# A chunked scan over two heads: from tiled products for each head to full-array products for a pair

## The chip, the core and the metric

The program runs on one core of one Trainium2 chip. The metric is the device time of one execution in microseconds. A core has TensorE (PE; its weight loads have a row of their own, PEld), VectorE (DVE), ScalarE (ACT), GpSimd (POOL) and SyncE (SP), each of which works through its own queue in order. SP, and in one place GpSimd, issue the DMAs.

## What is computed

Two decoder layers of width 2048 run over one sequence of 256 tokens. The first layer's token mixer is an RWKV-7 time mix with 32 heads of 64 channels, the second's is a convolution module; each is followed by a gated MLP. The change lies in the time mix, in the scan over tokens, which is cut here to its core:

```python
def step(S, inp):
    r_t, w_t, k_t, v_t, a_t, b_t = inp
    sa = jnp.einsum('bhij,bhj->bhi', S, a_t)
    S = (S * w_t[:, :, None, :] + sa[..., None] * b_t[:, :, None, :]
         + v_t[..., None] * k_t[:, :, None, :])
    y = jnp.einsum('bhij,bhj->bhi', S, r_t)
    return S, y
_, ys = lax.scan(step, S0, (r, decay, k, v, a, b))   # 256 steps, 32 heads
```

The state S is 64x64 for each head. Everything is float32.

## The kernel before

The kernel does the scan by chunks: 256 tokens are four chunks of 64 (`L`, `NC_`), and inside a chunk the recurrence is a triangular system, which is solved with matrix products. A tile of 128 partitions holds a **pair of heads**, head 0 in partitions 0 to 63 and head 1 in 64 to 127; there are 16 pairs.

Ahead of the scan the small triangular matrices of all heads (`dN`) are loaded by a GpSimd DMA (line 582), inverted in 32x32 blocks on VectorE (`inv_step`), and written back as `dT` and `dTn` by GpSimd DMAs (lines 640, 644). Meanwhile TensorE computes the first eight value tiles (`v_tile`). In the scan three kinds of work are interleaved:

- **Preparation of a pair** (`prep_gen`). For each chunk, one stationary operand holds the b and k vectors of both heads, and is multiplied with each head's a and r vectors (line 699, with the other head's rows zero) and with the identity (line 700, which gives the transpose). ScalarE copies a corner (`n21`, line 701) and the transpose (`tk`, line 706) out, VectorE masks the rest (line 704, 705). Then come eight 32x32 products `n21` by `tn` (line 714), eight centring products of the values, 64 columns at a time (line 733), and eight 32x32 products into the inverse's off-diagonal block (line 742). A bonus product follows (line 748). Each 32x32 or 64-column product uses a part of the array, which is chosen by where its operands and its output lie.
- **The chain of a pair** (`chain_gen`), chunk after chunk: W (line 762, a product for each head with 64 output rows), a ScalarE copy of W, the triangular product of both heads (line 775, full array), two ScalarE copies into `uv` (line 777), the state's update (line 781, one product for each head, then VectorE at line 161 or 786), and two contributions to the output y (lines 770 and 788, one product for each head). Each float32 product of a row is two instructions in the profile.
- **Filler**: value tiles 8 to 15 (`v_gen`, lines 244 to 246, three products of 256 columns for each of 16 blocks, from weights that ScalarE and GpSimd split into two parts), normalisation (`gn_gen`, tiled products at 798 and 816), first tiles of the output projection (`wo_gen`), and background jobs (`ada`, line 210, on VectorE, from weights of 1 MB).

PE's order is written by hand: a heap of generators, each with a due time, `PD` = 13 units a pair; the chains of two pairs and the preparation of a third are under way at a time. The other engines' orders are set by a scheduler. Loads of a pair (`prep_load`, `prep_load2`) stand on SP one pair ahead: `ari` (a and r, one tile for each head, zeros in the other head's partitions), `bk`, `tt` and `tn`. The zeros of `ari` that preparation overwrites are set again by GpSimd (line 765).

## Time and profile before

| | us |
|---|---|
| median of 3 runs | 2658.42 (2649.9 to 2659.04) |
| the profiled execution | 2656.6 |
| its span, first to last instruction | 2654.8 |
| the stretch from 400 to 720 us, in which the scan lies | 320 |
| PE busy in that stretch | 276.55 |
| VectorE / ScalarE / GpSimd busy in that stretch | 230.78 / 171.61 / 139.29 |
| granted TensorE clock, mean over the span | 0.975 |

In the PE timeline a row gives the start of the first instruction, the time to the end of the last, and a count. Ends overlap the next start, so what an instruction occupies is read from start to start. `128*64` ahead of the operands' shapes is the part of the array, rows by columns, that a product takes.

### The profile page before, as it was taken

The page shows a single profiled execution, that of the slowest core. Times are in us where ns is not written, and L with a number is a line of the kernel's source. Part 1 is how long each engine was busy: PE and PEld are TensorE (multiplying, and loading weights), DVE is VectorE, ACT ScalarE, POOL GpSimd, SP SyncE. Part 2 cuts the span into 40 slices and gives each one's busy share as a digit, 9 for nine tenths or more (in the row PEclk, how much of TensorE's full clock was granted, in tenths as well). Part 3 has the DMA queues.
Part 4 walks back from the last instruction along what each step waited for, and adds up shares of the span by engine and source line. Part 5 has one row for each costly group of instructions (what it writes and reads, how often), then busy time and mean ns, then how long its engine had stood idle before and what let it go on. Part 6 is the DMA issues. An engine that isn't in the chain of part 4 may idle for free.

```text
span 2654.8 us, 45461 instructions
## 1 busy us (share of the span) xinstructions
PE 2490.2 (94%) x17378; PEld 2202.6 (83%) x17378; DVE 2053.5 (77%) x3763; ACT 1363.4 (51%) x2636; POOL 507.2 (19%) x484
## 2 busy tenths in 40 slices
PE   5899997988999999999999989978999999999997
PEld 3688886877798888888888779967888888888886
DVE  4567767777678889889888989979998866666666
ACT  4565623565656543554455445544575445544554
POOL 0000016554002012002100248964320000000000
PEclk8999998999999999999999989979999999999999
DMA  8887766777275778888877854445767855555553
GB/s 316 323 319 277 202 214 213 230 222 231 98 270 218 283 282 340 299 295 300 323 289 286 289 201 159 160 143 213 265 237 279 282 197 187 179 191 190 191 178 124
DMA packets 154778, 630.37 MB, mean 237 GB/s; under 512 B 60480, under 2 KB 72256, under 8 KB 95936
## 3 DMA queue, kind: packets, MB, share of 16 engines
q1 hardware_dynamic: 153824, 624.85, 66.3%
q8 instruction: 136, 2.23, 0.3%
q0 software_dynamic: 736, 2.62, 0.3%
q14 instruction: 82, 0.67, 0.1%
HBM read 614.30 MB, written 13.11 MB: 236 GB/s over the span
## 4 chain that ended last, share of the span: by engine, by line
PE 71%; DVE 13%; DMA 9%; ACT 3%; issue 2%; POOL 1%; SPq 1%; DVEq 0%; ACTq 0%; POOLq 0%
PE ps L241 28%; PE ps L242 14%; PE ps L244 6%; PE ps L246 6%; PE ps L245 6%; DMA raw<-ada 5%; DVE raw L210 4%; DVE s L161 2%; DVE lo L234 2%; PE ps L379 1%; PE ps L307 1%; DVE s L158 1%; POOL lo L234 1%; ACT hi L233 1%; DVE s L155 1%
## 5 line engine op out<-in xcount | busy, mean ns | idle before, releaser
L241 PE MATMUL ps<-s,hi 128*128 128x512 f32 x3872 | 1357.5, 395 | 1.3 <-DVE s L155 1.1
L233 ACT CAST hi<-raw 128x1024 fp32r<-128x1024 f32 (+6 forms) x873 | 768.8, 897 | 862.4 <-PE ps L241 450.8
L242 PE MATMUL ps<-s,lo 128*128 128x256 f32 x3872 | 1086.0, 281 | 11.7 <-DVE lo L234 11.5
L234 DVE TENSOR_TENSOR lo<-raw,hi 128x1024 fp32r<-128x1024 f32 (+4 forms) x639 | 750.5, 1177 | 302.7 <-ACT hi L233 300.3
L241 PEld LDWEIGHTS ps<-s,hi 128*128 128x128 f32 x3872 | 726.5, 188 | 169.6 <-DVE s L155 1.7
L242 PEld LDWEIGHTS ps<-s,lo 128*128 128x128 f32 x3872 | 730.5, 189 | 18.8 <-DVE lo L234 17.4
L244 PE MATMUL ps<-s,hi 128*128 128x256 f32 (+1 forms) x1712 | 503.8, 295 | 7.3 <-ACT hi L233 5.6
L246 PE MATMUL ps<-s,lo 128*128 128x256 f32 (+1 forms) x1712 | 491.0, 288 | 19.3 <-DVE lo L234 17.2
L234 POOL TENSOR_TENSOR lo<-raw,hi 128x512 fp32r<-128x512 f32 x234 | 342.9, 1490 | 817.4 <-ACT hi L233 775.2
L245 PE MATMUL ps<-s,hi 128*128 128x256 f32 (+1 forms) x1712 | 489.7, 286 | 0.0
L246 PEld LDWEIGHTS ps<-s,lo 128*128 128x128 f32 x1712 | 330.5, 193 | 26.7 <-DVE lo L234 19.9
L244 PEld LDWEIGHTS ps<-s,hi 128*128 128x128 f32 x1712 | 330.7, 193 | 16.2 <-ACT hi L233 7.6
L245 PEld LDWEIGHTS ps<-s,hi 128*128 128x128 f32 x1712 | 331.2, 193 | 3.7 <-issue 3.0
L210 DVE CUSTOM_DVE_ANT_0 raw<-raw,cb,par 128x1024 f32<-128x1024 f32 x156 | 209.3, 1342 | 73.5 <-DMA raw<-ada 72.2
L210 DVE CUSTOM_DVE_ANT_0 raw<-raw,cb,md 128x1024 f32<-128x1024 f32 x156 | 217.1, 1392 | 0.8
L161 DVE SCALAR_TENSOR_TENSOR s<-ps,par,s 128x239 f32<-128x239 f32 (+26 forms) x420 | 166.0, 456 | 1.8 <-ACT s L164 1.2
L1192 POOL TENSOR_TENSOR s<-s,t 128x256 f32<-128x256 f32 x6 | 4.1, 726 | 703.5 <-DVE t L334 703.5
L161 DVE SCALAR_TENSOR_TENSOR s<-ps,md,s 128x256 f32<-128x256 f32 x213 | 100.7, 479 | 24.5 <-PE ps L242 19.6
L161 DVE SCALAR_TENSOR_TENSOR t<-t,par,t 128x255 f32<-128x255 f32 (+1 forms) x172 | 84.4, 491 | 1.1
L158 DVE TENSOR_TENSOR s<-ps,cst 64x64 f32<-64x64 f32 (+2 forms) x208 | 48.1, 253 | 34.5 <-ACT n L701 23.7
L164 ACT ACTIVATE t<-t,par 128x256 f32<-128x256 f32 x118 | 67.8, 585 | 7.0 <-DVE t L152 3.4
L155 DVE TENSOR_TENSOR s<-t,s 128x256 fp32r<-128x256 f32 x150 | 67.8, 461 | 1.5
(208 smaller groups left out, 2433.8 us busy)
## 6 DMA issues: line engine op xcount, KB each, us to landing
raw<-w_up SPq DMA_DIRECT2D x172, 1024.0 KB, 4.9
raw<-ada SPq DMA_DIRECT2D x156, 1024.0 KB, 6.4
raw<-w_dn SPq DMA_DIRECT2D x64, 896.0 KB, 4.6
raw<-w_pw SPq DMA_DIRECT2D x48, 1024.0 KB, 4.8
raw<-w_rkv SPq DMA_DIRECT2D x38, 1024.0 KB, 5.9
raw<-ada_s SPq DMA_DIRECT2D x32, 1024.0 KB, 6.6
raw<-w_dn SPq DMA_DIRECT2D x32, 960.0 KB, 6.2
raw<-w_o SPq DMA_DIRECT2D x11, 1024.0 KB, 5.0
```

The source lines that it names most:

```text
L155: nc.vector.tensor_tensor(out=o, in0=x, in1=y, op=ALU.subtract)
L158: nc.vector.tensor_tensor(out=o, in0=x, in1=y, op=ALU.mult)
L161: nc.vector.scalar_tensor_tensor(out=o, in0=x, scalar=s, in1=y, op0=op0, op1=op1)
L164: nc.scalar.activation(out=o, in_=i, func=func, bias=bias, scale=scale)
L210: nc.vector.tensor_tensor_reduce(out=r[q], in0=r[q], in1=cb[:, q * w:(q + 1) * w], scale=1.0, scalar=mod(l, piece, f) if q else pc("ada_b" ...
L233: nc.scalar.copy(hi[:, s], v[:, s])
L234: (eng or nc.vector).tensor_tensor(out=lo[:, s], in0=v[:, s], in1=hi[:, s], op=ALU.subtract)
L241: nc.tensor.matmul(acc.rearrange("p (a t) -> p a t", a=2), lhsT=hi[:, c], rhs=x[:, :, :T], start=first, stop=False, skip_group_check=True)
L242: nc.tensor.matmul(acc[:, T:], lhsT=lo[:, c], rhs=x[:, 0, :T], start=False, stop=last, skip_group_check=True)
L244: nc.tensor.matmul(acc[:, :n], lhsT=hi[:, c], rhs=x[:, 0, :n], start=first, stop=False)
L245: nc.tensor.matmul(acc[:, :n], lhsT=hi[:, c], rhs=x[:, 1, :n], start=False, stop=False)
L246: nc.tensor.matmul(acc[:, :n], lhsT=lo[:, c], rhs=x[:, 0, :n], start=False, stop=last)
```

## The change

Both heads of a pair are put side by side in the columns of one operand, with zeros where a head's columns meet the other head's rows. So each pair of products becomes one product of 128x128, of which the two diagonal 64x64 blocks are read.

- `ari` now is one tile for a (both heads) and one for r, in place of one for each head. Each is loaded by two DMAs, of 256-byte pieces: four for a pair where there were two of 2-KB pieces.
- W, both y products and the state's product are one full-array product each. The results lie in different columns for the two heads, so the copy of W becomes two copies of 64x64, and the copy of y two of 64x256. The square of y (`sqs`) is taken of the copy.
- The line-714 and line-742 products become four full-array products each, of 64 and of 96 columns, on `z` and on `tn` with zeros (two static buffers each, where `tn` had three).
- The centring becomes four products of 128 columns, on two neighbouring chunks of v; the last takes chunks 3 and 0, which GpSimd copies side by side into `vw`. The copies into `uv` become three.
- GpSimd sets a 64x64 block of `uv` to zero for each head.
- The identity product of line 700 becomes a transposing instruction (`nc.tensor.transpose`).
- Two switches that chose ScalarE and GpSimd forms (`WACT`, `RKP`) go; the forms stay.

```diff
-    aris = [[slot512().rearrange("p (c j t) -> p c j t", c=NC_, j=2) for _ in range(2)] for _ in range(4)]
+    aris = [[slot512().rearrange("p (c h t) -> p c h t", c=NC_, h=2) for _ in range(2)] for _ in range(4)]
...
+    zs = [pool.tile([P, NC_, 2, L], F32, tag="z", bufs=2, name=nm("z")) for _ in range(2)]
+    tns = [pool.tile([P, NC_, 2, 32], F32, tag="tn", bufs=2, name=nm("tn")) for _ in range(2)]
+    for t in zs + tns:
+        nc.gpsimd.memset(t, 0.0)
...
         for h, hr in enumerate(hrs):
-            nc.sync.dma_start(out=ari[h][hr], in_=dAR[f, hr])
+            for j in range(2):
+                nc.sync.dma_start(out=ari[j][hr, :, h, :], in_=dAR[f, hr, :, j, :])
...
+        for h, hr in enumerate(hrs):
+            nc.gpsimd.memset(uv[hr, 0, h, :], 0.0)
...
-            for h in range(2):
-                nc.tensor.matmul(pg[:, h * P:(h + 1) * P], lhsT=bkc, rhs=ari[h][:, c].rearrange("p j t -> p (j t)"), start=True, stop=True, skip_group_check=True)
-            nc.tensor.matmul(pg[:, T:T + P], lhsT=bkc, rhs=ident, start=True, stop=True, skip_group_check=True)
-            nc.scalar.copy(n21[:, c], pgv[:, :, 0, 32:64])
+            for j in range(2):
+                nc.tensor.matmul(pg[:, j * P:(j + 1) * P], lhsT=bkc, rhs=ari[j][:, c].rearrange("p h t -> p (h t)"), start=True, stop=True, skip_group_check=True)
+            nc.tensor.transpose(out=pg[:, T:T + P], in_=bkc, identity=ident)
+            nc.scalar.copy(z[:, c, :, 32:64], pgv[:, 0, :, 32:64])
...
-                nc.tensor.matmul(py[r1, c * 32:c * 32 + 32], lhsT=n21[r0, c, h, :], rhs=tn[r0, c, :], start=True, stop=True, skip_group_check=True)
+            nc.tensor.matmul(py[:, c * L:c * L + L], lhsT=z[:, c].rearrange("p h t -> p (h t)"), rhs=tn[:, c].rearrange("p h t -> p (h t)"), start=True, stop=True, skip_group_check=True)
...
-                nc.tensor.matmul(pvt[orow, cs], lhsT=v[:, cs], rhs=cen[:, hr], start=True, stop=True, skip_group_check=True)
+        vw = pool.tile([P, P], F32, tag="vw", bufs=1, name=nm("vw"))
+        for i, c in enumerate((NC_ - 1, 0)):
+            nc.gpsimd.tensor_copy(vw[:, i * L:(i + 1) * L], v[:, c * L:c * L + L])
+        for c in range(NC_):
+            vc = v[:, c * L:c * L + P] if c < NC_ - 1 else vw
+            nc.tensor.matmul(pvt[:, c * P:(c + 1) * P], lhsT=vc, rhs=cen, start=True, stop=True, skip_group_check=True)
...
-                nc.tensor.matmul(py[r0, c * 32:c * 32 + 32], lhsT=ysb[r1, c, :], rhs=tt[r1, c, r1], start=True, stop=True, skip_group_check=True)
+            nc.tensor.matmul(pyv[:, c], lhsT=z[:, c].rearrange("p h t -> p (h t)"), rhs=tt[:, c, 32:P], start=True, stop=True, skip_group_check=True)
...
-            for h, hr in enumerate(hrs):
-                kr = slice(0, P) if c else hrs[1 - h]
-                nc.tensor.matmul(pch[hr, wc], lhsT=ari[h][kr, c, 0, :], rhs=uv[kr, c, h, :], start=True, stop=True, skip_group_check=True)
+            nc.tensor.matmul(pch[:, wc], lhsT=flat(ari[0]), rhs=uvc, start=True, stop=True, skip_group_check=True)
...
-            (nc.scalar.copy if WACT else nc.vector.tensor_copy)(W, pch[:, wc])
+            for h, hr in enumerate(hrs):
+                nc.scalar.copy(W[hr], pw[hr, h])
...
-                for h, hr in enumerate(hrs):
-                    nc.tensor.matmul(psy[hr, cs], lhsT=uv[:, c, h, :], rhs=ari[h][:, c, 1, :], start=True, stop=False, skip_group_check=True)
+                nc.tensor.matmul(psy[:, cs], lhsT=uvc, rhs=flat(ari[1]), start=True, stop=False, skip_group_check=True)
...
-                for h, hr in enumerate(hrs):
-                    nc.tensor.matmul(pch[hr, wc], lhsT=tk[:, h, c, :], rhs=uv[:, c, h, :], start=True, stop=True, skip_group_check=True)
+                nc.tensor.matmul(pch[:, wc], lhsT=tk[:, c], rhs=uvc, start=True, stop=True, skip_group_check=True)
...
-            for h, hr in enumerate(hrs):
-                nc.tensor.matmul(psy[hr, cs], lhsT=uv[:, c, h, :], rhs=gr[:, h, c, :], start=c == 0, stop=True, skip_group_check=True)
+            nc.tensor.matmul(psy[:, cs], lhsT=uvc, rhs=flat(gr), start=c == 0, stop=True, skip_group_check=True)
...
-        nc.scalar.copy(ycs[f], psy[:, :T])
-        act(sqs[f], psy[:, :T], AF.Square)
+        for h, hr in enumerate(hrs):
+            nc.scalar.copy(ch(ycs[f])[hr], psv[hr, :, h, :])
+        act(sqs[f], ycs[f], AF.Square)
```

The lines of the changed kernel are numbered otherwise: 766, 774, 779, 784 and 790 are the chain's products (before: 762, 770, 775, 781, 788); 718, 735 and 744 are the preparation's (before: 714, 733, 742); 772 is the copy of W (before: 767); 732 is the copy into `vw`. Outside the scan each engine's order stays as it was.

Order on PE, one place in the scan where two chains, the centring and a block product meet. `ps` is an accumulator, `s` a data tile, `cst` the constants, `t` a value tile. Before:

```order
L762 MATMUL ps_4979<-s_4715,s_3976 64x64
L762 MATMUL ps_4979<-s_4715,s_3977 64x64
L770 MATMUL ps_4978<-s_3976,s_4715 64x64
L770 MATMUL ps_4978<-s_3977,s_4715 64x64
L733 MATMUL ps_5123<-cst,t_4126 64x64 x8
L762 MATMUL ps_4769<-s_4518,s_3974 64x64
L762 MATMUL ps_4769<-s_4518,s_3975 64x64
L770 MATMUL ps_4768<-s_3974,s_4518 64x64
L770 MATMUL ps_4768<-s_3975,s_4518 64x64
L742 MATMUL ps_5142<-s_3971,ys_5085 32x32 x8
L775 MATMUL ps_4979<-W_5117,s_3970 128x64
```

The same place in the changed kernel:

```order
L766 MATMUL ps_4962<-s_4713,s_3976 128x128
L774 MATMUL ps_4961<-s_3977,s_4713 128x128
L735 MATMUL ps_5096<-cst,t_4144 128x128 x3
L735 MATMUL ps_5096<-cst,vw_5097 128x128
L766 MATMUL ps_4768<-s_4528,s_3974 128x128
L774 MATMUL ps_4767<-s_3975,s_4528 128x128
L744 MATMUL ps_5114<-s_3971,z_4001 128x96 x4
L779 MATMUL ps_4962<-W_5090,s_3970 128x64
```

The steps stand in the same sequence; 24 tiled products became 12 full-array ones.

Order on ScalarE, the copies of one chain step between two chunks of preparation (`Sp` is the scaled state, `n` is `n21`, `t` and the second `s` are other copies). Before:

```order
L767 COPY W_4753<-ps_4555 128x64
L706 COPY s_4714<-ps_4733 128x2x64
L767 COPY W_4772<-ps_4769 128x64
L701 COPY n_804_4716<-ps_4774 128x64
L777 COPY s_4355<-ps_4555 64x64 x2
```

The changed kernel:

```order
L772 COPY W_4752<-ps_4567 64x64 x2
L713 COPY s_4712<-ps_4733 128x128
L772 COPY W_4770<-ps_4768 64x64 x2
L708 COPY z_4000<-ps_4773 128x2x32
L781 COPY s_4374<-ps_4567 64x64 x2
```

Each copy of W is two copies in a row. Over the whole program ScalarE has 2734 instructions for 2638, GpSimd 565 for 489, SP 992 for 960, and VectorE 3765 as before.

Order on GpSimd around the inversion, from the last zeros of `ari` to the first write of `dTn`; the `lo` rows split the weights of a value tile. Before:

```order
L610 MEMSET s_3979 64x512
L582 DMA raw_3963<-dN 128x1024 x2
L234 ISA
L234 TENSOR_TENSOR lo_4381<-raw_4365,hi_4380 128x512 x2
L234 TENSOR_TENSOR lo_4429<-raw_4365,hi_4428 128x512 x2
L644 DMA dTn<-s_4338 128x512
```

The changed kernel:

```order
L610 MEMSET s_3979 64x4x64 x2
L732 COPY vw_4501<-t_4029 128x64 x2
L580 DMA raw_3963<-dN 128x1024 x2
L232 ISA
L232 TENSOR_TENSOR lo_4400<-raw_4384,hi_4399 128x512 x2
L232 TENSOR_TENSOR lo_4448<-raw_4384,hi_4447 128x512 x2
L649 DMA dTn<-s_4358 128x512
```

The copies of pair 0's value chunks now stand ahead of the load of `dN` on this queue.

## Rows read from the trace of the kernel before

**Rows 1.** The profile page: the span.
```profile
span 2654.8 us, 45461 instructions
```

**Rows 2.** Stretches of the scan: length, then busy us (instructions) of PE, PEld, DVE, ACT, POOL; clock.
```profile
460.00:500.00 40.00, 39.70 (x461) 35.64 (x461) 27.70 (x80) 23.89 (x87) 25.63 (x21) 1.00 0.76 250
...
580.00:620.00 40.00, 33.45 (x400) 26.25 (x397) 34.97 (x95) 26.19 (x96) 19.33 (x22) 0.96 0.66 214
...
400.00:720.00 320.00, 276.55 (x2949) 232.66 (x2947) 230.78 (x598) 171.61 (x590) 139.29 (x126) 0.94 0.61 198
```

**Rows 3.** PE in time order (start, length, line, shapes, count): the array in one form.
```profile
479.76 0.61 PE L699 MATMUL ps<-s,s 128*128 128x128 f32 x4
480.21 0.39 PE L700 MATMUL ps<-cst,s 128*128 128x128 f32 x2
480.35 0.37 PE L244 MATMUL ps<-s,hi 128*128 128x256 f32 x1
480.55 0.28 PE L245 MATMUL ps<-s,hi 128*128 128x256 f32 x1
```

**Rows 4.** PE in time order: the six trips of tiled products in one head pair's period.
```profile
475.57 0.28 PE L246 MATMUL ps<-s,lo 128*128 128x256 f32 x1
475.78 0.33 PE L762 MATMUL ps<-s,s 64*64 64x64 f32 x4
...
476.27 0.28 PE L245 MATMUL ps<-s,hi 128*128 128x256 f32 x1
...
477.10 0.28 PE L246 MATMUL ps<-s,lo 128*128 128x256 f32 x1
...
478.24 0.39 PE L700 MATMUL ps<-cst,s 128*128 128x128 f32 x2
...
482.96 0.28 PE L246 MATMUL ps<-s,lo 128*128 128x256 f32 x1
483.17 0.34 PE L781 MATMUL ps<-s,s 128*64 128x64 f32 x4
483.34 0.29 PE L788 MATMUL ps<-s,s 128*64 128x64 f32 x4
...
483.78 0.28 PE L245 MATMUL ps<-s,hi 128*128 128x256 f32 x1
...
484.25 0.28 PE L246 MATMUL ps<-s,lo 128*128 128x256 f32 x1
484.46 0.44 PE L714 MATMUL ps<-tn,n 32*32 32x32 f32 x16
...
485.43 0.28 PE L245 MATMUL ps<-s,hi 128*128 128x256 f32 x1
...
485.91 0.28 PE L246 MATMUL ps<-s,lo 128*128 128x256 f32 x1
...
486.40 0.92 PE L733 MATMUL ps<-cst,t 128*64 128x64 f32 x16
...
487.73 0.44 PE L742 MATMUL ps<-s,ys 32*32 32x32 f32 x16
...
488.38 0.65 PE L748 MATMUL ps<-t,cst 128*128 128x256 f32 x2
488.86 0.33 PE L775 MATMUL ps<-W,s 128*128 128x64 f32 x2
...
489.98 0.38 PE L699 MATMUL ps<-s,s 128*128 128x128 f32 x1
```

**Rows 5.** Who waited for whom, 440 to 720 us: total us, times, longest.
```profile
PEld ps L775 <- ACT W L767: 6.4, 10, 1.5
```

**Rows 6.** ScalarE in time order: a copy of W.
```profile
477.69 0.21 ACT L767 COPY W<-ps 128x64 f32<-128x64 f32 x1 [0.57 <-PE ps L762]
```

**Rows 7.** ScalarE's copies of the first v tiles: min/median/max ns, first and last start us.
```profile
L590 ACT COPY t<-ps x8: 372/372/373, 359.6 to 407.9; 128x256 f32<-128x256 f32 x8
```

**Rows 8.** GpSimd in time order: the load of dN, with which the inversion begins.
```profile
365.02 1.26 POOL L582 DMA_DIRECT2D raw<-dN  x2 [9.25 <-DMA dN<-s]
```

More of the change, by code (lines that the diff above doesn't have):

```diff
@@ L64 @@
 BGT2 = 7
-WACT = 1
 TQ = 2
@@ L70 @@
 GP = 8
-RKP = 1
 NG = 12
@@ L668, in prep_load2 @@
         tt = tts[f % 4]
-        tn = pool.tile([P, NC_, 32], F32, tag="tn", bufs=3, name=nm("tn"))
+        tn = tns[f % 2]
         for h in range(2):
@@ L674, in prep_load2 @@
                 nc.sync.dma_start(out=tt[r0:r0 + 32, :, r0:r0 + 32], in_=dT[rows, b].rearrange("c s t -> s c t"))
-            nc.sync.dma_start(out=tn[h * L:h * L + 32], in_=dTn[rows].rearrange("c s t -> s c t"))
+            nc.sync.dma_start(out=tn[h * L:h * L + 32, :, h, :], in_=dTn[rows].rearrange("c s t -> s c t"))
         ld[f] += (tt, tn)
@@ L726, in prep_gen @@
+            nc.gpsimd.tensor_tensor(out=ch(rk)[hr], in0=ch(rk)[hr], in1=ari[1][hr, :, h, :], op=ALU.mult)
         yield PU
         pvt = ps("g")
-        for h, hr in enumerate(hrs):
-            orow = hrs[1 - h]
-            for c in range(NC_):
-                cs = slice(c * L, c * L + L)
-                nc.tensor.matmul(pvt[orow, cs], lhsT=v[:, cs], rhs=cen[:, hr], start=True, stop=True, skip_group_check=True)
-        for h, hr in enumerate(hrs):
-            orow = hrs[1 - h]
-            nc.scalar.copy(uv[orow, :, h, :], ch(pvt[orow, :T]))
+        vw = pool.tile([P, P], F32, tag="vw", bufs=1, name=nm("vw"))
@@ L737, in prep_gen @@
+        nc.scalar.copy(uv[hrs[1], 0, 0, :], pvv[hrs[1], NC_ - 1, 0, :])
         yield PU
         py = ps("g")
+        pyv = py[:, :NC_ * 96].rearrange("p (c t) -> p c t", c=NC_)
         for c in range(NC_):
[L740 to L742 removed]
+            nc.tensor.matmul(pyv[:, c], lhsT=z[:, c].rearrange("p h t -> p (h t)"), rhs=tt[:, c, 32:P], start=True, stop=True, skip_group_check=True)
```

55 lines of the change are left out of this document (26 added, 29 removed).

## The prediction

> **What bounds the kernel now.** I read the page first: PE is the engine that sets the end of the whole program, and the span is 2654.8 us [rows 1]; the profiled execution took 2656.6. The change touches only the scan, so I next read busy time by stretch [rows 2]. From 400 to 720 us PE is busy 276.55 of 320. Two kinds of stretch are to be seen. From 460 to 500 PE is busy 39.70 of 40 at full clock: there every nanosecond that PE's own stream saves or costs moves the end. From 580 to 620 it is busy 33.45: there it waits for VectorE, which is itself busy 34.97 of 40 with chain steps and background jobs, and a shorter PE stream only waits longer. After the scan PE goes on without a break into weights that are loaded ahead, so what the scan gains or loses reaches the end whole.
>
> Then I read PE in time order, from start to start. In one array form the stream is regular: four line-699 instructions of 128 columns take 480.21 - 479.76 = 0.45, so 0.112 each, and the step from them to the next kind costs nothing: 480.21 to 480.55 is 0.34 for two of line 700 and the first of line 244, which is 2 x 0.112 + 0.118 [rows 3]. So a full-array product of 128 columns (two instructions) costs 0.224, and a 256-column instruction of the value tile 0.118.
>
> A tiled product between them costs more than its instructions. One line-762 pair alone, between 475.57 and 476.27, takes 0.70; less the two 0.118 of its neighbours this is 0.46 [rows 4]. Lines 781 and 788 together, 482.96 to 483.78, take 0.82 - 0.236 = 0.58. So a further pair of head products costs 0.12 (its four 64-column instructions run beside one another), and the trip out of the full array and back costs 0.46 - 0.12 = 0.34, whatever is done in it.
>
> **The change part by part.**
>
> *Products and trips.* I add up one head pair's period, from 475 to 490 us, in which PE never waits [rows 4]. It has six trips with 14 pairs of head products, eight and eight 32x32 products and eight centring products:
> - 475.57 to 476.27: 0.46, as above.
> - 477.10 to 478.24: 1.14, less 0.118 and less 4 x 0.112 for the line-699 instructions in it: 0.57.
> - 482.96 to 483.78: 0.58.
> - 484.25 to 485.43: 1.18 - 0.236 = 0.94 (the line-714 products stand in it).
> - 485.91 to 488.38: 2.47, less 0.118 and some 0.2 for the line-775 product in it: 2.15 (centring, line 742 and two chain steps).
> - 488.86 to 489.98: 1.12, less 0.2 for line 775: 0.92; the cost of the way back comes after the last row shown, some 0.1.
>
> Sum: 5.72 us a pair. After the change the same work is 14 products at 0.224 (3.14), four centring products at 0.224 (0.90), and the four products of 64 and four of 96 columns. No row has these two shapes with a full-width output in a stream of their own. By columns they are 0.112 and 0.168, and no more than the 0.224 of 128 columns; I take the middle, 0.17 and 0.19: 1.45. Sum 5.49, so **-0.23 a pair, -3.7 us** for 16. With the low ends it is -9.0, with the high ends +1.7.
>
> *Trips that stay.* The products of lines 798 and 816 remain tiled: 16 and five groups. By the PE timeline about nine of these 21 now share a trip with head products and will have one of their own: 9 x 0.34 = **+3.1 us**.
>
> *The transposing instruction.* There are 64, each now a product of 0.224. No transposing instruction is in this trace. The nearest rows: unchanged, 0.224; one instruction of 128 columns in place of two, 0.112; the rate of the value tile's instructions (256 columns in 0.118), 0.06. I take 0.112, which differs least from the row it replaces: **-7.2 us** (0 to -10.5). It could also be a change of form with a trip's price of 0.34 each: +21.8; that is a rival. A sentence apart: the Trainium skill ("TensorE: Matmul & The Clock Gate", Terms) says that transposing is four times faster for float32, by which this term would be an estimated -10.8, and the sum 3.6 lower.
>
> *The copies of W.* ScalarE now copies W in two steps; one copy is 0.21 [rows 6], and I take the same for one of half the partitions. W is what the chain's full-array product waits for, and behind that PE's whole stream. PE's loads were seen to wait for this copy 10 times [rows 5]; in the other 54 chunks filler hides it. So 10 x 0.21 = **+2.1 us**, between 0 and 64 x 0.21 = 13.4. In all ScalarE gets 96 more instructions, some 20 us at 0.21; it is busy 171.61 of 320 [rows 2], and the weight splits that queue behind are made a tile ahead, so I cost the rest at nothing; if the cover is gone it is the first rival below.
>
> *What is given back.* The PE terms add up to -7.8. About two thirds of the scan is like 580 to 620, where PE waits for others anyway; I let half of the gain there go into longer waits: **+2.6 us**. What is late there is VectorE's state update behind a background job, which the change does not touch: VectorE has the same 3765 instructions.
>
> *SP.* 32 more DMA issues, in smaller pieces. They stand a pair's period (15 us) ahead of their use, so nothing waits for them, and behind them on SP are weight loads, also a tile ahead: 0. With two `tn` buffers in place of three the load for pair f waits for pair f-2's first block product, done by then: 0.
>
> *GpSimd.* 32 copies into `vw`, 32 zeroings of `uv`, and zeroings at the start. Pair 0's copies stand ahead of the load of `dN`, with which the inversion begins, and behind that load is the whole scan. They wait for the first value tile, whose copy starts at 359.6 and takes 0.37 [rows 7]; the load was issued only at 365.02, after 9.25 of waiting for the writes of `dN` [rows 8]. So there are 5 us of cover: 0. If the value tile came later than 364, each microsecond of it would be one of the end. In the scan GpSimd is busy 139.29 of 320 [rows 2], and `vw` is needed by the centring only late in a preparation: 0.
>
> Sum: -3.7 + 3.1 - 7.2 + 2.1 + 2.6 = -3.1, so 2656.6 - 3.1 = 2653.5 on the profiled execution. That execution lies 1.8 below the median of the three runs, 2658.4; against the median the sum gives 2655.3. I forecast **2654**.
>
> **The rivals.**
>
> *All of it is cheap.* The transposing instruction at 0.06, the narrow products by their columns, W's second copy hidden: -9.0 + 3.1 - 10.5 = -16.4, if PE's gain is felt everywhere: 2640. For it speaks that a tiled trip also delays what the chain waits for; against it the stretches in which VectorE is late.
>
> *ScalarE becomes the bound of the chain.* If each of its 96 added copies is on the path (20.2) and transposing gains nothing: 20.2 - 3.7 + 3.1 = +19.6, 2676. It decides from the point where ScalarE is busy most of the time between two chain steps; it is busy 171.61 of 320 now, which speaks against it.
>
> *Transposing drains the array as a tiled product does.* 64 x 0.34 = +21.8, with -3.7 + 3.1 + 2.1: +23.3, 2680. It would show as a step of some 0.3 around each transposing row; nothing in this trace speaks for or against it.
>
> *The trip's price is not that of the form.* If the 0.34 stayed when the products fill the array (because the chain's operands cost it), the old work without trips is 5.72 - 6 x 0.34 = 3.68, the new 5.49: 1.81 x 16 = +29.0, less 7.2, plus 2.1: 2680. Against it: line 699 follows line 246 and line 244 follows line 700 at no price [rows 3]. Beside it, a sentence apart: the Trainium skill ("TensorEngine Tiling (Array Packing)", Theoretical Speedup and Key Properties) says that 64-wide tiles work in parallel for up to twice the speed, which speaks against this change, and that a switch of the tiling mode drains the array, which speaks for it; the trace agrees with both, 0.12 for two heads' products against 0.224, and 0.34 a trip.
>
> **How the numbers follow.** Half a per cent, 13 us, is about what a measurement of this kernel tells from no change: 2645 to 2672. The forecast's case, terms of either sign that nearly cancel, has 0.50. All cheap has 0.28 and is the case of faster by more than that. ScalarE 0.11, draining 0.08 and the trip's price 0.03 are the slower cases, 0.22. The range reaches from the cheap case, with 6 us beyond its centre for waits that shrink too, to the slower rivals' centres: 2634 to 2680; what is left out is some of either tail, under 2 in 10.
>
> **What would show it.** On PE's timeline the chain's products should stand at 0.22 with no step before or after; the `z` products between 0.11 and 0.22 each; the transposing row at 0.11. PE's busy share from 460 to 500 should stay near full with the pair's period of about 15 us shorter by 0.5. PE's waits for W should grow by about 2 us, and those for VectorE a little. The load of `dN` should be issued as soon after its writes as before. I am wrong if PE's waits in the scan change by more than 10 us either way, or if a step of 0.3 stands at each transposing row.

## The result, and the profile after the change

The changed kernel takes **2684.24 us** (median of four runs, 2675.34 to 2686.33) against 2658.39 for the kernel before: a ratio of 1.0101, with a 95% interval of 1.008 to 1.0122. Run again beside the experiments it came to 2679.82, ratio 1.0099 (1.0077 to 1.0121). It is slower by about 26 us. The forecast was 2654, with a range that ended at 2680, so the prediction was wrong in sign and just missed with its range.

The profiled execution took 2683.13 us. First its span and the stretches that answer to [rows 1, 2] (columns as there):

```profile
span 2681.4 us, 43888 instructions
```

```profile
460.00:500.00 40.00, 35.41 (x274) 33.23 (x272) 25.59 (x68) 23.42 (x87) 23.57 (x27) 0.96 0.68 220
580.00:620.00 40.00, 33.48 (x244) 30.35 (x243) 30.92 (x88) 26.52 (x107) 11.08 (x24) 0.91 0.65 205
400.00:720.00 320.00, 277.32 (x1980) 253.44 (x1979) 222.48 (x581) 184.28 (x653) 145.02 (x188) 0.93 0.63 201
```

From 460 to 500 us PE was busy 39.70 of 40 before and is now busy 35.41: the stretch that I took for one bound by PE alone has become one in which PE waits. Over 400 to 720 PE is as busy as before (277.32 against 276.55), but the scan is not over at 720.

To see both sides I cut the scan the same way in every trace, from pair 0's bonus product (line 748 before, 750 after) to the last product of W with the inverse (line 775 before, 779 after), and added up for each PE instruction the time to the start of the next, less the idle time that the trace shows between them. I call the sum PE's work in the scan.

| us in the scan | before | after | after, second execution |
|---|---|---|---|
| length | 265.6 | 284.6 | 280.4 |
| PE's work | 241.2 | 254.3 | 253.4 |
| of it, at the lower granted clock | 14.8 | 21.9 | 19.5 |
| PE's work, all at the higher clock (estimate) | 235.0 | 244.3 | 244.4 |
| PE idle | 24.4 | 30.3 | 27.1 |

The second execution is the changed kernel run again. The trace shows the clock granted to PE at one of two levels in each stretch, 1.2 or 2.4 GHz. Over the whole program the mean granted clock is the same, 0.974 against 0.975, but in the scan it is 0.966 before and 0.958 and 0.963 after. At the lower level an instruction of the same line and shape, with the same line behind it, occupied PE 1.7 to 1.9 times as long as at the higher; the estimate divides the work at the lower level by that (1.72 before, 1.83 and 1.85 after).

So 15 to 19 us of the loss lie in the scan: some 9 in PE's work as such, 3 to 4 in that more of it ran at the lower clock, 3 to 6 in idle time. With one execution of the kernel before, it isn't shown that the change itself brings the lower clock: in the scans of the runs below that have the background products, it lasts from 6 to 55 us. The rest of the loss lies ahead of the scan and behind it, where the executions shown here differ by several us anyway (pair 0's bonus product starts between 433.6 and 447.5 in them).

What PE waited for, 440 to 725 us (total us, times, longest), before and then after:

```profile
PE ps L762 <- DVE s L161: 5.5, 7, 1.7
PE ps L775 <- ACT W L767: 3.9, 7, 1.2
```

```profile
PE ps L766 <- DVE s L159: 16.4, 11, 4.4
PE ps L779 <- ACT W L772: 1.9, 4, 0.7
```

The wait for the copy of W, now in two steps, did not grow. The wait of the W product for VectorE's state update (line 161 before, 159 after) tripled; in the second execution it is 13.0. What stands ahead of that update is to be seen in VectorE's time order, after:

```profile
478.38 1.28 DVE L208 CUSTOM_DVE_ANT_0 raw<-raw,cb,par 128x1024 f32<-128x1024 f32 x1 [5.66 <-issue]
...
480.66 1.48 DVE L208 CUSTOM_DVE_ANT_0 raw<-raw,cb,md 128x1024 f32<-128x1024 f32 x1
482.06 0.08 DVE L208 DVE_READ_ACCUMULATOR2_ANT md<- 128x1 f32 x1
482.06 0.58 DVE L159 SCALAR_TENSOR_TENSOR s<-ps,plc,Sp 64x64 f32<-64x64 f32 x2
```

Line 208 is a background product: half of a modulation vector's dot product, which runs on VectorE beside the scan. VectorE stood idle 5.66 us at the head of one, then ran both halves, and only then the state update. The profile names no releaser for that wait (`issue`), but the load of these weights was issued at 472.76 and took 5.5 us to land. PE's W product is what waited:

```profile
482.70 0.56 PE L766 MATMUL ps<-s,s 128*128 128x128 f32 x2 [2.61 <-DVE s L159]
```

VectorE's waits ahead of such products, before and after (same columns as the waits above; 16.6 and 5.9 in the second execution):

```profile
DVE raw L210 <- DMA raw<-ada: 15.7, 15, 2.8
```

```profile
DVE raw L208 <- DMA raw<-ada: 24.4, 12, 5.4
...
DVE raw L208 <- issue: 10.5, 3, 5.7
```

Now the prices. PE in time order after, a stretch with weight tiles between the trips:

```profile
469.32 0.28 PE L244 MATMUL ps<-s,lo 128*128 128x256 f32 x1
469.44 0.39 PE L784 MATMUL ps<-s,s 128*128 128x128 f32 x2
469.66 0.39 PE L790 MATMUL ps<-s,s 128*128 128x128 f32 x2
469.81 0.36 PE L242 MATMUL ps<-s,hi 128*128 128x256 f32 x1
470.01 0.28 PE L243 MATMUL ps<-s,hi 128*128 128x256 f32 x1
...
470.48 0.28 PE L244 MATMUL ps<-s,lo 128*128 128x256 f32 x1
470.60 1.00 PE L718 MATMUL ps<-tn,z 128*128 128x64 f32 x8
471.44 0.44 PE L784 MATMUL ps<-s,s 128*128 128x128 f32 x2
471.71 0.39 PE L790 MATMUL ps<-s,s 128*128 128x128 f32 x2
471.85 0.36 PE L242 MATMUL ps<-s,hi 128*128 128x256 f32 x1
472.06 0.28 PE L243 MATMUL ps<-s,hi 128*128 128x256 f32 x1
```

State and y product of a chunk (lines 784, 790) between weight tiles: 469.32 to 470.01 is 0.69, against 0.82 in [rows 4] from 482.96 to 483.78, a gain as forecast. With the first y products beside them: 470.48 to 472.06 is 1.58, against 1.18 in [rows 4] from 484.25 to 485.43, a loss of 0.40, where the prediction's own prices make 0.18. Line 718 shows why: its eight instructions are 64 columns wide, and the next line starts 0.84 later, 0.105 each, nearly what 128 columns take.

### The profile page after: what moved, and what is told of

It reads as the page before. It is cut to its first block, busy times and chain, and to the rows that moved or that the text cites. A ratio compares the mean times of both kernels' runs of the same rounds, so it can differ in the third digit from the quotient of the medians.

```text
span 2681.4 us, 43888 instructions
## 1 busy us (share of the span) xinstructions
PE 2512.5 (94%) x16482; PEld 2234.6 (83%) x16482; DVE 2049.1 (76%) x3763; ACT 1387.0 (52%) x2732; POOL 517.5 (19%) x560
## 4 chain that ended last, share of the span: by engine, by line
PE 69%; DVE 13%; DMA 9%; ACT 3%; issue 3%; POOL 1%; SPq 1%; DVEq 0%; ACTq 0%; POOLq 0%
PE ps L239 27%; PE ps L240 14%; PE ps L242 6%; PE ps L244 6%; PE ps L243 6%; DMA raw<-ada 5%; DVE raw L208 4%; DVE lo L232 3%; DVE s L159 2%; PE ps L377 1%; ACT hi L231 1%; DVE s L156 1%; DMA raw<-w_dn 1%; POOL lo L232 1%; DVE s L153 1%
## 5 line engine op out<-in xcount | busy, mean ns | idle before, releaser
L244 PE MATMUL ps<-s,lo 128*128 128x256 f32 (+1 forms) x1712 | 491.6, 288 | 18.5 <-DVE lo L232 17.9
L232 POOL TENSOR_TENSOR lo<-raw,hi 128x512 fp32r<-128x512 f32 x234 | 336.0, 1460 | 816.9 <-ACT hi L231 759.1
L244 PEld LDWEIGHTS ps<-s,lo 128*128 128x128 f32 x1712 | 330.5, 193 | 26.3 <-DVE lo L232 20.8
L159 DVE SCALAR_TENSOR_TENSOR s<-ps,md,s 128x256 f32<-128x256 f32 x213 | 100.8, 480 | 30.3 <-PE ps L240 20.8
L162 ACT ACTIVATE t<-t 128x256 f32<-128x256 f32 x118 | 49.2, 417 | 55.1 <-DVE t L159 50.2
```

The lines of the kernel that those rows point to most:

```text
L159: nc.vector.scalar_tensor_tensor(out=o, in0=x, scalar=s, in1=y, op0=op0, op1=op1)
L162: nc.scalar.activation(out=o, in_=i, func=func, bias=bias, scale=scale)
L232: (eng or nc.vector).tensor_tensor(out=lo[:, s], in0=v[:, s], in1=hi[:, s], op=ALU.subtract)
L244: nc.tensor.matmul(acc[:, :n], lhsT=lo[:, c], rhs=x[:, 0, :n], start=False, stop=last)
```

## The experiments

Theory A: the loss is PE's work. Theory B: it is the order on VectorE, where a state update stands behind a background product that waits for its weights. Theory C: a full-width step takes longer from state to W and back. D: SP's extra issues. E: GpSimd, held by the one buffer of `vw`. Each ratio is against the kernel before, timed on the same chip.

### Each part alone, or put back alone

**The transposing instruction alone**, in the kernel before:

```diff
-nc.tensor.matmul(pg[:, T:T + P], lhsT=bkc, rhs=ident, start=True, stop=True, skip_group_check=True)
+nc.tensor.transpose(out=pg[:, T:T + P], in_=bkc, identity=ident)
```

> The kernel before with one edit: the product with the identity becomes a transposing instruction. Theory A (TensorE's work sets the scan): in the trace of the changed kernel the transposing takes 5.5 us in the scan where the product took 13.6, so 8 us less work for TensorE; if half to all of that reaches the end, 2650 to 2655 us against 2658. Theory B (the changed kernel is slow because background products on VectorE come ahead of the chain's state update, not because of TensorE's work): within 3 us of 2658, either way. Rival of the prediction (the transposing instruction drains TensorE): 2680.

2658.75 us, ratio 1.0011 (0.9994 to 1.0028). As B had it. PE's work in the scan fell by 5.6 us (its own line by 6.4) and idle time rose by 2.5; of the rest no gain is to be seen in the whole time. PE in time order there:

```profile
478.42 0.71 PE L699 MATMUL ps<-s,s 128*128 128x128 f32 x4
478.97 0.27 PE L700 MATMUL ps<-cst,s 128*128 128x128 f32 x1
479.00 0.37 PE L244 MATMUL ps<-s,hi 128*128 128x256 f32 x1
```

From the four of line 699 to the weight tile is 0.58, and five instructions of 0.112 would be 0.56: no step of 0.3 stands there.

**The changed kernel with its y products put back** into 32x32 tiles:

```diff
-nc.tensor.matmul(py[:, c * L:c * L + L], lhsT=z[:, c].rearrange("p h t -> p (h t)"), rhs=tn[:, c].rearrange("p h t -> p (h t)"), start=True, stop=True, skip_group_check=True)
+for h in range(2):
+    r0, r1 = slice(h * L, h * L + 32), slice(h * L + 32, h * L + 64)
+    nc.tensor.matmul(py[r1, c * 32:c * 32 + 32], lhsT=z[r0, c, h, 32:64], rhs=tn[r0, c, h, :], start=True, stop=True, skip_group_check=True)
...
-nc.tensor.matmul(pyv[:, c], lhsT=z[:, c].rearrange("p h t -> p (h t)"), rhs=tt[:, c, 32:P], start=True, stop=True, skip_group_check=True)
+for h in range(2):
+    r0, r1 = slice(h * L, h * L + 32), slice(h * L + 32, h * L + 64)
+    nc.tensor.matmul(py[r0, c * 32:c * 32 + 32], lhsT=z[r1, c, h, 0:32], rhs=tt[r1, c, r1], start=True, stop=True, skip_group_check=True)
...
```

> The changed kernel with the two y products of the preparation put back into 32x32 tiles of the array (z and tn keep their new layout). Theory A: over the scan these products take 15.7 + 15.0 us of TensorE's time after and took 7.1 + 7.0 before, so 16.6 us of work goes, and two of six trips per pair come back (16 pairs x 2 x 0.09 to 0.34 us = 2.9 to 10.9 us): 2684 - 6 to 14 = 2670 to 2678 us. Theory B: TensorE's work is not what counts, 2681 to 2688 us.

2669.47 us, ratio 1.0051 (1.0032 to 1.007): about half of the loss is gone. PE's work fell by 7.7 (y lines 14.9 less, 7.2 back elsewhere for two trips a pair). That is half a microsecond under A's band and far from B's: B alone is out.

**The changed kernel with centring put back** into half width, without `vw`:

```diff
-vw = pool.tile([P, P], F32, tag="vw", bufs=1, name=nm("vw"))
...
-    nc.tensor.matmul(pvt[:, c * P:(c + 1) * P], lhsT=vc, rhs=cen, start=True, stop=True, skip_group_check=True)
+for h, hr in enumerate(hrs):
+    orow = hrs[1 - h]
+    for c in range(NC_):
+        cs = slice(c * L, c * L + L)
+        nc.tensor.matmul(pvt[orow, cs], lhsT=v[:, cs], rhs=cen[:, hr], start=True, stop=True, skip_group_check=True)
...
```

> The changed kernel with the centring products of v put back into half-width products, two of 64 columns for a chunk, so that the wrap tile vw and its two GpSimd copies are gone. Theory A: centring took 14.6 us of TensorE's time before and 16.9 after, and two of six trips come back: 2684 give or take 5 (2680 to 2689). Theory B in the form that GpSimd, held by the single vw tile (20.8 us of waits for the centring product in the scan), makes the low halves of the weights and with them the next loads late: at least 8 us less, 2676 or under.

2668.72 us, ratio 1.0052 (1.0036 to 1.0068). A expected no change; B, in the form in which GpSimd is held by `vw`, expected 2676 or under. PE's work is only 2 us less, and that by the clock (by the estimate at the higher clock it is 1 more); its idle time is 7 less (23.1). So A alone is out too.

**The changed kernel with the chain put back** into half width:

```diff
-nc.tensor.matmul(pch[:, wc], lhsT=flat(ari[0]), rhs=uvc, start=True, stop=True, skip_group_check=True)
+for h, hr in enumerate(hrs):
+    kr = slice(0, P) if c else hrs[1 - h]
+    nc.tensor.matmul(pch[hr, wc], lhsT=ari[0][kr, c, h, :], rhs=uv[kr, c, h, :], start=True, stop=True, skip_group_check=True)
...
-for h, hr in enumerate(hrs):
-    nc.scalar.copy(W[hr], pw[hr, h])
+nc.scalar.copy(W, pch[:, wc])
...
```

The state product and both y products are put back in the same way.

> The changed kernel with the chain's products (W, y, state, y of u) put back into half-width products, W in one ScalarE copy and the output tile in its old layout; the preparation stays full-width. Theory A: these lines took 47.8 us of TensorE's time in the scan before and 58.0 after, so 10 us of work goes and two of six trips per pair come back (2.9 to 10.9 us): 2684 - 7 to +1 = 2677 to 2685 us. Theory B in the form that the chain's own steps (W's two copies, a state product that ends later) start the lag of the state updates: at least 12 us less, 2672 or under.

2665.01 us, ratio 1.0032 (1.0011 to 1.0054), in B's band. PE's work is not less at all (258.2 against 254.3; the chain's lines 9.4 less, the trips back, and 2 us more by the clock), but its idle time fell from 30.3 to 13.0. Against 2684 and 2680 the three edits give back 10 to 15, 11 to 16 and 15 to 19 us: their sum is far more than the whole loss, so the parts don't add up in the time.

**The chain alone** at full width, the preparation as before: the changed kernel with its y products, its centring and the product with the identity put back, by the diffs shown.

> Only the chain's four products take the full array (W, both y products, state), with W in two copies; y products, centring and the product with the identity are as in the kernel before. Theory A: the chain's lines took 9 us more of TensorE's time in the changed kernel, and the trips they saved come off, so 2658 + 5 to 12 = 2663 to 2670 us. Theory C: the idle time grows by 5 us or more on top of that, 2670 to 2677.

2668.55 us, ratio 1.0039 (1.0022 to 1.0055), where A put it. C isn't seen: PE's idle time in the scan, 21.3, is no longer than before.

**The new layout alone**: the changed kernel with its y products, its centring and its chain put back by the three diffs. The transposing instruction stays.

> Every full-width product is put back, and what is left of the change is the layout: ari's two tiles by use with both heads in each, four small loads of dAR per pair for two, tn in two buffers for three, tk's single copy, the memsets of uv, and the transposing instruction. Theory A: these cost nothing, within 4 us of the run with the transposing instruction alone, 2655 to 2663 us. Theory D (the queue of SP: four small loads take longer to issue, so later weights land late): 2665 us or more.

2654.52 us, ratio 0.9991 (0.9973 to 1.0009). SP's smaller loads, two `tn` buffers and the zeroings cost nothing that can be measured. D falls.

Taken at the higher clock by the same estimate, PE's work in the scan is 6.5 us less than before with the transposing instruction alone, 5.8 more with the chain alone, and 6.4 less with the new layout; against the changed kernel it is 8.4 less with the y products put back, 1.2 more with centring and 2.0 more with the chain.

### Without the background products

The kernels of this part leave 34 of the products out, so they compute less than the task.

```diff
-at(0, bg_gen(99))
+for l_, piece, f in jobs:
+    nc.gpsimd.tensor_copy(out=mod(l_, piece, f), in_=pc("ada_b", (l_ * 6 + piece) * KT + f))
...
+del jobs[:]
```

> The kernel before without the 34 modulation products (of the o gate and of the FFN's scale and shift) that run in the scan's background on VectorE, and without their 34 loads; their columns hold the bias alone. It is the base for the next run. From the first bonus product to the last u product the kernel before takes 265.6 us, of which TensorE is idle for 24.4; here, if VectorE's queue is what TensorE waits for, the idle time falls to 12 us or less.

> The same edit in the changed kernel, which leaves out the same 34 products and loads. With them the changed kernel took 284.6 us from the first bonus to the last u product (254.3 us of work for TensorE and 30.3 idle) against 265.6 (241.2 and 24.4). Theory A: the 13 us of work stay, and the two kernels differ by 11 to 16 us in this stretch. Theory B (order on VectorE): TensorE's idle time comes out equal in both, within 2 us, since nothing stands ahead of the state updates. Theory C (a full-width step takes longer from the state to W and back, so that TensorE waits on the chain itself): the changed kernel still idles 5 us or more longer than the one before.

| us in the scan, no background products | before | after |
|---|---|---|
| length | 239.0 | 249.1 |
| PE's work | 233.3 | 241.3 |
| PE idle | 5.7 | 7.8 |

PE's idle time before, 5.7, is less than half of the 12 that I allowed. The difference between the kernels fell from 15 to 19 us to 10: 8 of work, 2 of idle time. Waits for the state update all but vanish, after without background products:

```profile
PE ps L766 <- DVE s L159: 1.2, 3, 0.5
```

The difference is 1 us short of A's band, and the idle time grew by just the 2 us that B allowed. So theories A and B both hold a part, and C at most the 2 us of idle time. How far the scan hangs on the background products is to be seen in the chain of waits of the kernel before, which I had not read for this stretch (shares by line, 440 to 707 us):

```profile
by line: DMA raw<-ada 17.9%; DVE raw L210 14.0%; PE ps L244 4.9%; PE ps L699 4.6%; DVE s L158 3.7%; PE ps L811 3.5%; DMA s<-dAR 3.5%; PE ps L245 3.5%; PE ps L246 3.4%; issue 3.2%; PE ps L762 2.7%; DMA raw<-w_o 2.6%; PE ps L775 2.6%; PE ps L
```

and without the background products (438 to 678 us):

```profile
by line: PE ps L699 13.0%; PE ps L244 11.3%; PE ps L245 7.7%; PE ps L246 7.6%; PE ps L775 6.1%; PE ps L811 5.7%; PE ps L762 5.7%; PE ps L700 5.3%; PE ps L781 5.0%; PE ps L733 4.0%; PE ps L788 3.7%; PE ps L816 3.4%; PE ps L748 3.3%; PE ps L7
```

Already before the change 32% of the scan's chain ran through the loads of the background products and the products themselves; take them away and it runs through PE. The share changes from one execution to the next: after the change it is 31% in the first and 19% in the second.

Timed, the two kernels:

> The kernel before without the 34 modulation products of the scan's background and without their loads, timed: 2621 us, give or take 6. It is the base for the next run.

> The changed kernel without the same 34 products and loads, timed beside the run before it. Theory A alone (the loss is TensorE's work, whatever runs beside it): the two differ by what the full kernels differ by, 22 to 28 us. Theories A and B together (8 us of work in the scan, and the rest comes from waits for the state update behind a background product): they differ by 6 to 14 us. Theory B alone: by less than 4 us.

2621.49 us, ratio 0.9874 (0.9847 to 0.99), and 2638.59, ratio 0.9942 (0.992 to 0.9964): 17 us apart, between the bands that I had set. The scans of these two profiles are 239.6 and 249.3 us long, within 0.6 of the first two, so the stretch repeats. The other 7 us of the medians I can't place: the two profiled executions are only 4 us apart (spans of 2628.5 and 2632.5).

With so steady a stretch the parts could be priced (same edits as above, background products left out):

> The kernel before with the transposing instruction, and without the 34 background products and their loads (left out of the computation, as in the base run). From the first bonus to the last u product the base takes 239.0 to 239.6 us (233.3 to 233.8 of work for TensorE). Theory A: work falls by 6 to 7 us and the stretch by 5 to 7, to 232 to 235 us, since nothing gives the gain back. If the gain was never there: 238 or more.

> Only the chain's products take the full array, without the same 34 background products and loads (left out). Theory A: W, state and y lines take 8.6 us more than in the base, and the trips that go give back 2 to 6: the stretch comes to 242 to 246 us. By the prediction's step (0.34 a trip, 0.224 a product, 0.12 a pair of half-width products) the chain would gain: 14 x 0.224 - 14 x 0.12 - 4 x 0.34 = +0.1 a pair, 239 to 242 us.

> The changed kernel with its y products back in 32x32 tiles, without the same 34 background products and loads (left out). The changed kernel without them takes 249.1 to 249.3 us. Theory A: 14.7 us of work goes and two trips a pair come back, 4 to 8 us: 239 to 243 us.

> The changed kernel with its centring products back in half width, without the same 34 background products and loads (left out). Theory A: 2 us of work goes, one trip a pair comes back, 2 to 5 us: 247 to 252 us. With the background products the same edit gave back 11 us or more; if centring has a cost of its own that TensorE's lines don't show, the stretch falls here too, to 243 or less. Theory B (the 11 us came from what stands before the state updates on VectorE): no such fall here.

| kernel, no background products | scan | PE's work | at the higher clock (estimate) | idle |
|---|---|---|---|---|
| before | 239.6 | 233.8 | 232.3 | 5.8 |
| before, transposing instruction | 233.8 | 227.5 | 225.6 | 6.3 |
| before, chain at full width | 246.0 | 237.9 | 237.9 | 8.1 |
| after | 249.3 | 241.4 | 239.8 | 8.0 |
| after, y products put back | 244.5 | 234.6 | 231.1 | 9.9 |
| after, centring put back | 250.6 | 242.8 | 241.2 | 7.8 |

In the scan's length transposing is worth 5.8 us here; the chain costs 6.4, where the prediction's prices gave 0 to 2; the y products cost 4.8, less than A's 6 to 10; centring gains 1.3. That makes 4.1 of the 9.7: here too the parts don't add up, in part by the clock. Taken at the higher clock, PE's work changes by 6.7 less, 5.6 more, 8.7 more and 1.4 less, nearly what the same edits did beside the background products (6.5, 5.8, 8.4, 1.2): PE's prices are the same in both settings. These four kernels ran once each, and as whole programs (2624.81, 2627.2, 2628.41 and 2646.69 us, in the order of the expectations) they don't show these differences: transposing has no gain over the base's 2621, and with centring put back the time is 8 to 14 us above the changed kernel's 2638.59 and 2632.59. Putting centring back gave 11 us or more with the background products and loses 1.3 without them: what it cost lies in what runs beside it, not in its own PE time.

Where the 10 us lie is shown by the pairs' periods (start of one pair's bonus product to the next, from the two timed kernels). Pairs 1 to 6, between whose products v's weight tiles stand: 99.5 us before, 100.1 after. From pair 7 to the end: 125.4 before, 136.7 after, and 8.1 of these 11.3 lie in pairs 7 to 10, which have no weight tile between their products. PE in time order in pair 8, the kernel before without background products (first execution):

```profile
567.32 0.34 PE L781 MATMUL ps<-s,s 128*64 128x64 f32 x4
567.48 0.29 PE L788 MATMUL ps<-s,s 128*64 128x64 f32 x4
567.70 0.44 PE L714 MATMUL ps<-tn,n 32*32 32x32 f32 x16
568.07 0.34 PE L781 MATMUL ps<-s,s 128*64 128x64 f32 x4
568.23 0.29 PE L788 MATMUL ps<-s,s 128*64 128x64 f32 x4
568.35 0.32 PE L762 MATMUL ps<-s,s 128*64 128x64 f32 x4
568.50 0.29 PE L770 MATMUL ps<-s,s 128*64 128x64 f32 x4
568.62 0.92 PE L733 MATMUL ps<-cst,t 128*64 128x64 f32 x16
569.40 0.34 PE L762 MATMUL ps<-s,s 128*64 128x64 f32 x4
569.57 0.29 PE L770 MATMUL ps<-s,s 128*64 128x64 f32 x4
569.78 0.44 PE L742 MATMUL ps<-s,ys 32*32 32x32 f32 x16
570.15 0.43 PE L775 MATMUL ps<-W,s 128*128 128x64 f32 x2
```

and the same work in the changed kernel without them:

```profile
563.74 0.27 PE L707 MATMUL ps<-cst,s 128*128 128x128 f32 x1
563.85 0.39 PE L784 MATMUL ps<-s,s 128*128 128x128 f32 x2
564.07 0.39 PE L790 MATMUL ps<-s,s 128*128 128x128 f32 x2
564.29 1.00 PE L718 MATMUL ps<-tn,z 128*128 128x64 f32 x8
565.13 0.44 PE L784 MATMUL ps<-s,s 128*128 128x128 f32 x2
565.41 0.39 PE L790 MATMUL ps<-s,s 128*128 128x128 f32 x2
565.85 0.49 PE L766 MATMUL ps<-s,s 128*128 128x128 f32 x2
...
567.74 1.03 PE L744 MATMUL ps<-s,z 128*128 128x96 f32 x8
568.60 0.36 PE L779 MATMUL ps<-W,s 128*128 128x64 f32 x2
```

Before, PE enters the tiled form once, at 567.32, and stays there until 570.15: 2.83 us. After, the same products take from 563.85 to 568.60: 4.75. Here there are no trips to save, and the heads' halves no longer run beside one another. The transposing row is one instruction, 563.74 to 563.85.

With the background products the loss lies elsewhere. From pair 7 to the end it is 144.0 before and 149.7 after (148.4 in the second execution), but pairs 1 to 6 grow from 105.7 to 120.8 (117.7). These six pairs, before and after (columns as in [rows 2]):

```profile
457.68:563.39 105.71, 99.06 (x1145) 86.06 (x1144) 79.27 (x196) 65.08 (x220) 67.15 (x59) 1.00 0.72 233
```

```profile
459.60:580.39 120.79, 106.94 (x810) 99.61 (x810) 76.95 (x196) 73.49 (x256) 69.78 (x84) 0.96 0.66 205
```

PE's idle time there went from 6.7 to 13.9 us (12.3), and 10.2 us of its work (6.8) ran at the lower clock, against none before. So what the background products add to the loss lies in these six pairs; from pair 7 on the loss is about half of what it is without them.

### What holds the background products up

**Two buffers for `vw`:**

```diff
-vw = pool.tile([P, P], F32, tag="vw", bufs=1, name=nm("vw"))
+vw = pool.tile([P, P], F32, tag="vw", bufs=2, name=nm("vw"))
```

> The changed kernel once more, unedited, as the base on the chip of the next three: 2684 us, give or take 5.

> The changed kernel with the wrap tile vw in two buffers in place of one. Theory E (GpSimd stands at the copy into vw until TensorE has read the pair before's, 20.8 us in six waits, and the low halves of weights queue behind it, so that loads and with them the background products come late): at least 6 us off, 2678 or under, as far as 2669, where the run without vw came out. Theory A (what centring costs is TensorE's time): no more than 4 us off, 2680 to 2688.

The changed kernel 2679.82, with two buffers 2681.61, ratio 1.0104 (1.008 to 1.0128): no gain. But GpSimd's wait at this copy is still 14.7 us (20.8 and 16.6 in the two executions with one buffer), so the run rules out the buffer and not GpSimd's queue:

```profile
POOL vw L732 <- PE ps L735: 14.7, 5, 8.9
```

**Background products in quarters**, in the changed kernel and in the kernel before with the transposing instruction:

```diff
-TQ = 2
+TQ = 4
```

> The changed kernel with each background product done in four pieces of 512 columns in place of two of 1024, so that a state update stands behind 0.7 us in place of 1.3. If the length of a piece is what delays the state updates, TensorE's waits for VectorE before W (17 us in the scan) fall by a third or more and the time by 4 to 8 us, to 2672 to 2678. If it is the wait for the weights at the head of VectorE's queue (30 to 36 us of idle time before these products, against 17 before the change), no gain: 2678 to 2688.

> The kernel before with the transposing instruction, whose 5.8 us without the background products were given back with them, and with the same four pieces. If the length of a piece gave the gain back: 2648 to 2653 us, ahead of both kernels. If the weights at the head of the queue did: 2655 to 2662.

2677.59, ratio 1.0066 (1.004 to 1.0092), and 2661.14, ratio 1.0017 (0.9996 to 1.0038). The first is 2 to 9 us less than the changed kernel, with intervals that overlap; yet PE's idle time stayed at 29.0 us and its wait for the state update at 13.4 (13.0 in the second execution of the changed kernel), so it isn't the mechanism that I had put. PE's work is 248.0, and by the estimate at the higher clock 245.3, no less than the changed kernel's: the lower clock lasted only 6.4 us of this scan. The second is no gain. Neither beats the kernel before, and no other run of the whole computation does by more than its interval.

```profile
PE ps L766 <- DVE s L159: 13.4, 12, 3.1
```

## Why the prediction was wrong, step by step

**What bounds the kernel: half right.** I read the bound from busy shares and from one stretch at 39.70 of 40. The chain of waits for the scan, which I did not read, puts 32% on the background products and their loads and no line of PE above 5%. A longer PE stream there is not only longer: it uses up its weight tiles later, the next loads start later, and VectorE stands at the head of a background product with a state update behind it. The runs show that a part of the loss, 5 to 9 us of the scan's 15 to 19, needs the background products, and that it stands as PE's idle time and lower clock, mostly in pairs 1 to 6; the way by which PE's stream delays their weights is only argued.

**Products and trips: the step that failed.** I had -3.7 us. Without background products the scan grows by 9.7 while transposing takes 5.8 off, so this term, with the trips that stay, W's copies and what PE waits for, is +15.5. In PE's work alone, taken at the higher clock, it is some +14 there (7.5 more in all, 6.7 less by transposing) and some +16 with the background products (9.3 and 6.5). This is what the runs show in place of the -3.7:
- *One pair stood for sixteen.* I counted six trips in a pair's period full of weight tiles [rows 4]. In that setting single steps came out as forecast (0.82 to 0.69, and a lone W from 0.70 to 0.46). But where no weight tile stands between, one trip holds nearly all of a pair's products, and the change replaces 2.83 us by 4.75. Without background products pairs 7 to 15 grow by 11.3 us, more than the whole 9.7, since pair 0 is 2.2 shorter. Even pairs 1 to 6 grew by 0.6, where this term and transposing had promised 4.1 less; the narrow products are some 2 of that, and the rest I can't name.
- *The narrow products.* I took 0.17 and 0.19 for 64 and 96 columns, the middle of a range. They cost 0.225 and 0.215 (13.5 and 12.9 us in 60 products each), the top of it. By columns was the wrong rule. That is some 5 us, and with the top of the range the term was still only +1.7. The Trainium skill ("TensorEngine Tiling (Array Packing)", Theoretical Speedup) gives up to four times for one dimension of at most 32 and up to 16 where both are small, which spoke against this part in particular. The trace has the direction, with a factor of 2.3: sixteen 32x32 instructions in 0.37 (567.70 to 568.07), the eight full-width ones that replace them in 0.84 (470.60 to 471.44).
- *The long trip: not the miss.* I took 2.15 us for centring, line 742 and two chain steps; at the prediction's prices the new work is 2.56 (0.90 + 0.76 + 4 x 0.224), 0.41 more. In the scans without background products this group grows by 0.53 where it stands between weight tiles without a wait (2.61 to 3.14 from tile to tile, two of each); 0.49 is line 744 against line 742 ((12.9 - 5.6) / 15 pairs).

**Trips that stay: not seen in full.** +3.1 was forecast; lines 798 and 816 took 11.1 us of PE's work before (2.3 + 8.8) and their successors 11.7. The way into a trip counts on the line before it and isn't in these sums.

**The transposing instruction: right in PE's time, wrong in the whole.** -7.2 was forecast; its line went from 12.8 to 5.4, and the instruction stands at 0.11, with no step beside it. The Trainium skill's four times for float32 ("TensorE: Matmul & The Clock Gate", Terms) doesn't show here: 0.11 against 0.224 is two times. In the scan without background products it was worth 5.8; with them the whole time didn't change.

**The copies of W: too dear.** +2.1 was forecast; PE's waits for W went from 3.9 to 1.9, and those of its weight loads, which the term was counted from, from 6.4 to 4.1. The rival in which ScalarE bounds the chain isn't seen.

**What is given back: too small, and of the wrong sign.** I let half of a gain go into waits for VectorE, "which the change does not touch". PE's stream grew instead, and the waits for VectorE grew with it, from 5.5 to 16.4 (13.0).

**SP and GpSimd at nothing: right** for SP (ratio 0.9991 with the new layout). The load of `dN`, against [rows 8]:

```profile
372.55 1.26 POOL L580 DMA_DIRECT2D raw<-dN  x2 [4.12 <-DMA dN<-s]
```

It waits for the writes of `dN`, as before, and so not for the copies into `vw`. In the scan GpSimd's part stays open: without `vw` the changed kernel was 11 us faster or more, with two buffers of it no faster.

**The rivals.** The slower ones had prices of 2676 and 2680 for other reasons; none was this one. A rival "the tiled products run beside one another where no weight tile separates them" would have been priced from the rows of pair 8. The sum of the last rival, 1.81 more a pair less 0.45 for transposing, is what PE's work in pairs 7 and 8 grew by, 1.3 each; its reason was another.

What stays open: how the 5 to 9 us that need the background products divide between GpSimd's queue, the loads' issue and VectorE's order, whether the lower clock follows from the waits, and where the part of the loss outside the scan comes from. A fifth tile for the loads wasn't tried.

## What to carry to other kernels

Count a change of form in more than one setting: a trip out of the full array has a price only where full-array work stands on both sides of it, and back to back the small tiles of both heads run beside one another, here for 0.6 of the time of the zero-filled products (2.83 for 4.75 us). Before a gain or a loss on the busiest engine is carried to the end one to one, read the chain of waits for that stretch: when a third of it belongs to background work and its loads, a microsecond saved may be lost there, and a microsecond added may cost more than one. And compare two traces' work on TensorE only after taking the granted clock of that very stretch into account, not the mean of the program.

## What the runs showed of the hardware

A float32 product with 64 or 96 moving columns and 128 stationary columns took as long as one with 128: 0.105 to 0.112 an instruction. Its weight load alone lasted 0.186 to 0.192, against 0.101 to 0.152 for a 32x32 tile, but I have no run that shows which of the two sets the 0.11. A transposing instruction of float32 took one pass of 0.11 in place of two, without a step before or after it. And 34 background products on VectorE with their loads cost the kernel before 33 us (2654.40 to 2621.49 on one chip), though VectorE has idle time in the scan. At the lower of its two granted clocks an instruction of TensorE occupied it 1.7 to 1.9 times as long as at the higher; the lower one lasted 17.9 us of the scan before the change, and 2.7 and 3.4 without those 34 products.
